# Twelve gate blocks of a hybrid decoder layer moved from the scan to the conv stage: Strassen pairs there, a denser scan here

## The chip, the cores and the metric

The kernel runs on one core of one Trainium2 chip. The metric is the device time of one execution in microseconds; before the change the median of three runs is 2601.65 us (2600.45 to 2602.65). Less is better.

## The reference, cut to what matters

One layer of a decoder works on 1024 prompt tokens and 8 sample tokens, 1032 columns in all, at model width 1024. A combined projection of the normed input gives the inputs of three mixers and their gates:

```
sc_b, sc_c, sc_x, z, xbc, dt_raw, q, gates = split(rmsnorm(x) @ w_in)
y_a = (sc_b * conv3(sc_c * sc_x)) @ w_sc_out
xs, B, C = split(silu(conv4(xbc) + bias))
y_ssd, state = chunked_scan(xs, softplus(dt_raw), a, B, C)      # 8 chunks of 128 tokens, 4 groups of 8 heads
y_b = group_rmsnorm((y_ssd + d * xs) * silu(z)) @ w_ssm_out
y_c = attention(q, mem_k, mem_v) @ w_attn_o
x += (sigmoid(gates) split in three, times y_a, y_b, y_c, summed) @ w_merge_o
x += (silu(n @ w_gate) * (n @ w_up)) @ w_down,  n = rmsnorm(x);   then a final rmsnorm
```

What the change touches is `gates`: 3072 columns of `w_in`, which are 24 blocks of 128, each followed by a sigmoid.

## The kernel before, in words

**Layout.** Activations lie transposed, 128 features by 1032 tokens, as eight pairs of tiles: a rounded fp32r part and the fp32r rest. Each weight block is split the same way, and each product is three matmuls (high by high, high by low, low by high).

**Plain block.** `gemm` (L180) makes 128 output columns: 8 k-steps of 3 matmuls of 3 column stretches of 344, so 72 matmuls at L192. At some k-steps (`marks`, L185) it calls `tick` (L168), which pops one piece of work from the queue `pend` and issues it; `pace[0]` (L178) sets how many pieces a block takes: 3, at k-steps 0, 2 and 5. `run_next` (L138) runs the next block from its queues, and loads the raw weights of the one after it first.

**Strassen pair.** `strassen` (L271) makes two blocks at once from seven products over half the k-range and half the tokens: 7 x 4 k-steps x 3 x 2 stretches of 258, so 168 matmuls at L236. VectorE makes sums of the weights, ScalarE and VectorE split them (L223, L224), and copies and additions join the products (L288 to L318). The sums of the activations (`xforms`) are made once.

**Order of the stages around the change.** First come the norm and six pairs of z blocks beside the memory keys (`z_pair`, L691). Then, at L1138 to L1158, come the *conv inputs*: eleven pairs of xbc blocks and one z pair, L1144. `xbc_pair` (L670) evicts the pair, runs the width-4 conv on VectorE (L595 to L601) and SiLU on ScalarE. Then the Strassen tiles close and the *scan* opens (L1164). Plain blocks are the main work there: a queue `fillers` of eight short-conv channels with three blocks each (`sc_step`, L603) and eight q blocks, and a queue `gates` of the 24 gate blocks (`gate_step`, L646). The 160 pieces of the scan stand in `pend`: per group 3 to load, 27 for the head and the chunks, 1 that loads z, 4 that multiply by z, 2 empty ones and 3 of the group norm, 40 in all.

**One chunk of the scan** is three pieces. p1 (`first`, L755) transposes B and x (L761, L765), multiplies C and B (L762), masks (L767, L770) and scales (L772, L776). p2 (`third`, L811) adds to the state (L815, L821), decays it on GpSimd (L828), works on a sample token (`s_step`, L873) and has ScalarE prepare the next decay matrix `r` (`prep`, L739: eight activations L742, then exp L743). p3 (`second`, L781) makes the output (L789 to L806). The matrix `r` is loaded by a broadcasting DMA of 512 KB, issued by SyncE (L736) two chunks ahead, into one of three tiles; loads, stores and weights share SyncE's queue, in order. Between two groups, `z_pieces` (L944) and `group_norm` (L973; psny L965, x L980, store yb_d L983) free the tiles into which the next group's x is loaded (L1183).

A Tile scheduler fixes each engine's order of instructions when the kernel is built, by its own estimate; it can move a piece's instruction a little later among the plain matmuls.

After the scan, the queue `gates` goes on into the *attention stage* (L1396 to L1443): what is left of the gate blocks, then three rounds of eight output blocks (`out_part`, L1420), beside the 69 pieces of the attention. These load 16 cache tiles `kc` (L1252) and their `qb` (L1249) through two buffers.

Of the kernel before, what the change touches and what calls it, by code (L numbers as in the profile page):

```python
# [11 lines left out]
AF = mybir.ActivationFunctionType  # L12
# [5 lines left out]
P = 128  # L18
# [3 lines left out]
TT = T + NS  # L22
# [15 lines left out]
C_SCB, C_SCC, C_SCX, C_Z, C_XBC, C_DT, C_Q, C_G = 0, 1024, 2048, 3072, 5120, 8192, 8224, 9248  # L38
# [3 lines left out]
def tile_kernel(ctx: ExitStack, tc, a, o):  # L42
    nc = tc.nc
    V, S, G, PE, SY = nc.vector, nc.scalar, nc.gpsimd, nc.tensor, nc.sync
# [22 lines left out]
    def dram(name, shape):  # L67
        return dp.tile(shape, F32, tag=name, name=name)

    def act_tile(part, name, dt=F32R, shape=(P, TT)):  # L70
        return ap_.tile(list(shape), dt, tag=part, name=name)
# [49 lines left out]
    def load_raw(src, name):  # L121
        raw = wp.tile([P, 1024], F32, tag="raw", name=name + "r")
        if len(src.shape) == 3:
            in_turn("raw", SY.dma_start(raw.rearrange("p (k c) -> p k c", k=src.shape[1]), src))
        else:
            in_turn("raw", SY.dma_start(raw, src))
        return raw
# [10 lines left out]
    def run_next(*queues):  # L138

        q = [f for d in queues for f in d]  # L140
        (queues[0] or queues[-1]).popleft()
        if len(q) > 1 and isinstance(q[1], Step):
            loaded[q[1].name] = load_raw(q[1].src, q[1].name)
        q[0]()
# [11 lines left out]
    def ev_tile(name, shape=(P, TT + 4), dt=F32):  # L156
        return ev.tile(list(shape), dt, tag="ev", name=name)
# [20 lines left out]
    pace = [3]  # L178
# [19 lines left out]
    def wblock(w, col):  # L198
        return w[:, col : col + P].rearrange("(k p) c -> p k c", p=P)
# [5 lines left out]
    HS = [slice(0, HT), slice(HT, TT)]  # L205
# [3 lines left out]
    def h3(t):  # L209
        return t.rearrange("p (n c) -> p n c", n=2)  # L210
# [125 lines left out]
    gt_d = dram("gt_d", [24, P, TT])  # L336
    mg_d = dram("mg_d", [KD, P, TT])
    xs_d = dram("xs_d", [24, P, TT])
    zs_d = dram("zs_d", [16, P, TT])
# [16 lines left out]
    w_in = a["w_in"][0]  # L356
# [12 lines left out]
    with tc.tile_pool(name="p0", bufs=1) as p0:  # L369
# [39 lines left out]
        def par(key, i):  # L409
            return prm[:, PC[key] + i : PC[key] + i + 1]  # L410
# [90 lines left out]
    def small(name):  # L501
        return pd_.tile([P, W], F32, tag=name, name=name)

    x0, mx, u, z, z2, q = (small(n) for n in ("x0", "mx", "u", "z", "z2", "q"))
# [141 lines left out]
    def gate_step(i):  # L646
        def s():
            ps = proj(C_G + i * P, f"g{i}")
            t = ev_tile(f"g{i}")
            S.activation(t3(t), flat(ps), AF.Sigmoid)  # L650
            S.dma_start(gt_d[i], t[:, :TT])

        return [Step(wblock(w_in, C_G + i * P), f"wg{i}", s)]

    def xbc_conv(ct, u, name):
        G.memset(u[:, 0:3], 0.0)
        G.tensor_copy(tail_xc[:, ct // 8, :, ct % 8], u[:, T : T + 11])
        acc = ev_tile("a" + name)
        conv(acc, u, h_xc, "xcw", ct, 24, 4, par("scb", ct))
        S.activation(acc[:, :TT], acc[:, :TT], AF.Silu)  # L660
        S.dma_start(xs_d[ct], acc[:, :TT])
# [8 lines left out]
    def xbc_pair(c1, c2, after_t3=None):  # L670
        us = []

        def outs():
            us.extend([pa_["u"](f"u{c1}"), pa_["u"](f"u{c2}")])
            return us[0][:, 3 : 3 + HT], us[0][:, 3 + HT : 3 + TT], None, us[1][:, 3 + HT : 3 + TT]

        pa = strassen(
            wblock(w_in, C_XBC + c1 * P), wblock(w_in, C_XBC + c2 * P), xforms, f"X{c1}", pa_["s"], outs,
            after_t3=after_t3,
        )  # L680
        xbc_conv(c1, us[0], f"x{c1}")
        S.activation(h3(us[1][:, 3 : 3 + HT]), pa, AF.Copy, scale=-1.0)
        xbc_conv(c2, us[1], f"x{c2}")
# [4 lines left out]
        S.activation(t3(t), flat(ps), AF.Silu)  # L688
        S.dma_start(zs_d[i], t[:, :TT])

    def z_pair(i):  # L691
        os = []

        def outs():
            os.extend([pa_["u"](f"z{i}"), pa_["u"](f"z{i + 1}")])
            return os[0][:, HS[0]], os[0][:, HS[1]], None, os[1][:, HS[1]]

        pa = strassen(
            wblock(w_in, C_Z + i * P), wblock(w_in, C_Z + (i + 1) * P), xforms, f"Z{i}", pa_["s"], outs
        )  # L700
        S.activation(os[0][:, :TT], os[0][:, :TT], AF.Silu)
        S.dma_start(zs_d[i], os[0][:, :TT])
        S.activation(os[1][:, HS[1]], os[1][:, HS[1]], AF.Silu)
        S.activation(h3(os[1][:, HS[0]]), pa, AF.Silu, scale=-1.0)
        S.dma_start(zs_d[i + 1], os[1][:, :TT])


    ssd = ExitStack()
# [230 lines left out]
    def z_load(g, t, hold):  # L939
        zs = act_tile(("ah", "al")[t % 2], f"zs{g}{t}", F32)  # L940
        SY.dma_start(zs, zs_d[g * 4 + t])
        hold[t] = zs

    def z_pieces(g, xg, hold):  # L944
        def piece(t):
            zs = hold.pop(t)
            V.tensor_mul(xg[t], xg[t], zs)
            if t == 0:
                hold["q"] = ev_tile(f"sqa{g}")
            sqa = hold["q"]  # L950
            if t == 0:
                S.activation(sqa[:, :TT], xg[t], AF.Square)
            else:
                S.activation(zs, xg[t], AF.Square)
                V.tensor_add(sqa[:, :TT], sqa[:, :TT], zs)
            if t + 2 < 4:
                z_load(g, t + 2, hold)

        return [lambda t=t: piece(t) for t in range(4)]

    def norm_chunk(sqa, i, n, r, v, name):

        c = slice(i * CW, (i + 1) * CW)
        ps = sm_ps(f"psn{name}{i}")
        PE.matmul(ps[:, :CW], ones, sqa[:, c], start=True, stop=True)  # L965
        V.tensor_scalar(v[:, c], ps[:, :CW], 1.0 / n, EPS, op0=ALU.mult, op1=ALU.add)
        S.activation(sqa[:, c], v[:, c], AF.Sqrt)
        V.reciprocal(r[:, c], sqa[:, c])
        V.tensor_mul(sqa[:, c], r[:, c], r[:, c])
        V.scalar_tensor_tensor(sqa[:, c], v[:, c], -0.5, sqa[:, c], op0=ALU.mult, op1=ALU.mult)  # L970
        V.scalar_tensor_tensor(r[:, c], sqa[:, c], 1.5, r[:, c], op0=ALU.add, op1=ALU.mult)

    def group_norm(g, xg, hold):  # L973
        def piece(i):
            if i == 0:
                hold["r"], hold["v"] = ev_tile(f"nr{g}"), ev_tile(f"nv{g}")
            norm_chunk(hold["q"], i, 512, hold["r"], hold["v"], f"y{g}")
            if i == NCH - 1:
                for t in range(4):
                    V.scalar_tensor_tensor(  # L980
                        xg[t], xg[t], par("ssn", g * 4 + t), hold["r"][:, :TT], op0=ALU.mult, op1=ALU.mult
                    )
                    SY.dma_start(yb_d[g * 4 + t], xg[t])  # L983

        return [lambda i=i: piece(i) for i in range(NCH)]

    def q_rows():
# [9 lines left out]
    pa_ = {"u": ev_tile, "s": lambda nm: ev_tile(nm, (P, 1024))}  # L997
# [4 lines left out]
    xforms = {  # L1002
        "B11": [tuple(t[:, HS[0]] for t in xn[k]) for k in range(4)],
        "B21": [tuple(t[:, HS[0]] for t in xn[k + 4]) for k in range(4)],
        "B22": [tuple(t[:, HS[1]] for t in xn[k + 4]) for k in range(4)],
        "T3": [tuple(t[:, HS[1]] for t in xn[k]) for k in range(4)],
        "T1": [], "nT2": [], "T4": [],
    }
# [128 lines left out]
    pa_["s"] = lambda nm: pxa.tile([P, 1024], F32, tag="s", name=nm) if nm[-1] == "a" else ev_tile(nm, (P, 1024))  # L1137
    xbc_pair(17, 21)  # L1138
    xbc_pair(0, 1)
    xbc_pair(2, 3)  # L1140
    xbc_pair(4, 5)
    xbc_pair(6, 7)
    xbc_pair(8, 9)
    z_pair(14)  # L1144
    xbc_pair(10, 11)
    xbc_pair(12, 13)
    xbc_pair(14, 15)
    rb = ev_tile("rb")
    SY.dma_start(rb[:, :TT], r_d.to_broadcast([P, TT]))
# [13 lines left out]

    pool["ssd"] = ssd.enter_context(tc.tile_pool(name="ssd", bufs=2))  # L1164
    gates = deque()
    for i in range(24):
        gates.extend(gate_step(i))
    fillers = deque()
    for ct in range(8):
# [3 lines left out]
    for g in range(GROUPS):  # L1173
        xg, bcg, hold = [], [], {}

        def load_group(g=g, xg=xg, bcg=bcg):
            for i, part in ((16, "ah"), (20, "al")):
                t = act_tile(part, f"bc{i}{g}", F32)
                SY.dma_start(t, xs_d[i + g])
                bcg.append(t)  # L1180
            for i in range(4):
                t = act_tile(("ah", "al")[i % 2], f"x{g}{i}", F32)
                SY.dma_start(t, xs_d[g * 4 + i])  # L1183
                xg.append(t)

        pieces = ssd_pieces(g, xg, bcg)
        pend.extend([load_group, None, lambda g=g, bcg=bcg: bc_rows(g, bcg)])
        pend.extend(pieces[:-3])
        pend.append(lambda g=g, hold=hold: [z_load(g, t, hold) for t in range(2)])
        pend.extend(pieces[-3:])  # L1190
        pend.extend(z_pieces(g, xg, hold) + [None] * 2 + group_norm(g, xg, hold))
    while pend:
        run_next(fillers, gates)


    assert not fillers
# [412 lines left out]
    for j in range(0, NF, 2):  # L1609
        s1, s2, pa = hidden_pair("g", j)  # L1610
# [3 lines left out]
        u1, u2, pa = hidden_pair("u", j)  # L1614
# [143 lines left out]
```

## Time and profile before

| what | us |
|---|---|
| median of 3 runs | 2601.65 |
| the profiled execution: its time / its span | 2603.75 / 2601.7 |
| TensorE busy / VectorE / ScalarE / GpSimd | 2521.7 / 1466.5 / 936.6 / 197.9 |
| mean granted TensorE clock | 0.988 |
| conv inputs, nine pairs, 314.7 to 496.8 | 182.1 |
| scan with its plain blocks, 540.5 to 1296.2 | 755.7 |
| DMA share in the scan | 0.60 |

The time of the profiled execution stands 2.1 above the median and its span 2.05 below that time. Times in the views are from the start of the span. A row of a view reads: start, duration, engine, line, operation, output <- inputs, partitions x elements; in brackets the idle time just before it and what ended it. "PE" is TensorE, "DVE" VectorE, "ACT" ScalarE, "POOL" GpSimd, "SPq" the DMA issues of SyncE. Durations of neighbouring matmuls overlap, so the distance of starts is their price. In a view of stages, each engine has its busy time and its count in brackets, and the row ends with the granted clock, the DMA share and GB/s.

### The profile page before, as it was taken

How to read it: one execution, taken by the hardware profiler on the slowest of the kernel's cores; microseconds unless marked ns; L12 is line 12 of the kernel's file. 1: busy time of each engine (PE TensorE's matmuls, PEld its weight loads, DVE VectorE, ACT ScalarE, POOL GpSimd, SP SyncE). 2: the span in 40 equal slices, each digit the busy share in tenths (PEclk: the TensorE clock that was granted, in tenths of full speed). 3: DMA queues.
4: the chain of work that ended last, by engine and by line, in shares of the span. 5: the costliest groups of instructions: out<-in, count | busy, mean ns of one | idle time of the engine just before them, and what ended most of it. 6: DMA issues, size and time to landing. Idle time of an engine off the chain costs nothing.

```text
span 2601.7 us, 42760 instructions
## 1 busy us (share of the span) xinstructions
PE 2521.7 (97%) x18037; PEld 2453.8 (94%) x18037; DVE 1466.5 (56%) x2037; ACT 936.6 (36%) x1434; POOL 197.9 (8%) x211
## 2 busy tenths in 40 slices
PE   7999999999998999999999999999989999999998
PEld 5899999999998999999999898999979999999998
DVE  5844586866667655555566633444784445454316
ACT  6643444553232235354342322213343333341202
POOL 0000000013213123023000000000010000000000
PEclk9999999999999999999999999999989999999999
DMA  6244333376556755665487757854322222265211
GB/s 190 94 138 156 124 104 106 123 206 148 154 157 138 161 185 160 176 196 150 133 292 243 273 175 252 299 173 144 122 73 82 74 90 66 82 212 163 66 41 66
DMA packets 391422, 389.31 MB, mean 150 GB/s; under 512 B 15622, under 2 KB 337782, under 8 KB 391223
## 3 DMA queue, kind: packets, MB, share of 16 engines
q1 hardware_dynamic: 372654, 335.74, 43.4%
q10 hardware_dynamic: 18577, 50.84, 5.1%
q8 instruction: 142, 2.33, 0.4%
q14 instruction: 49, 0.40, 0.0%
HBM read 280.41 MB, written 106.34 MB: 149 GB/s over the span
## 4 chain that ended last, share of the span: by engine, by line
PE 68%; DMA 5%; DVE 4%; issue 1%; ACT 1%; SPq 0%; POOL 0%; ACTq 0%; DVEq 0%; POOLq 0%
PE ps_g L192 10%; PE po L192 10%; PE pd L192 8%; PE ps_scc L192 4%; PE pm L1535 4%; PE ps_q L192 4%; PE ps_scx L192 3%; PE ps_scb L192 3%; DMA kc<-in_cache_mem_k_dram 1%; PE py L797 1%; PE pss L815 1%; PE po L789 1%; DMA r<-ac_d 1%; PE u20m L236 1%; PE g20m L236 1%
## 5 line engine op out<-in xcount | busy, mean ns | idle before, releaser
L1658 DVE TENSOR_TENSOR x<-pd,x 128x1032 f32<-128x1032 f32 x24 | 29.5, 1231 | 131.4 <-PE pd L192 131.4
L742 ACT ACTIVATE r<-r,acum 128x128 f32<-128x128 f32 x256 | 78.9, 391 | 36.2 <-DMA r<-ac_d 34.8
L1424 DVE TENSOR_TENSOR gt<-po,gt 128x1032 f32<-128x1032 f32 x24 | 29.5, 1230 | 70.4 <-PE po L192 69.1
L776 POOL TENSOR_TENSOR xdd<-xdt,decst 128x512 f32<-128x512 f32 x32 | 46.6, 1456 | 268.1 <-DVE xdt L772 268.1
L1583 POOL TENSOR_TENSOR x<-x,x 128x516 f32<-128x516 f32 x4 | 8.9, 2235 | 635.8 <-DVE x L1502 635.8
L598 DVE SCALAR_TENSOR_TENSOR ax<-u,prm,ax 128x1024 f32<-128x1024 f32 x44 | 56.4, 1281 | 0.3 <-ACT ax L595 0.3
L882 POOL TENSOR_TENSOR st<-st,xb 128x512 f32<-128x512 f32 x32 | 43.8, 1368 | 36.2 <-DVE xb L876 34.0
L769 ACT COPY bT<-bp 128x128 f32<-128x128 f32 x32 | 8.5, 264 | 105.4 <-DVE cbm L767 105.4
L770 DVE TENSOR_TENSOR r<-r,cbm 128x1024 f32<-128x1024 f32 x32 | 39.1, 1222 | 8.6 <-ACT r L743 8.0
L806 DVE SCALAR_TENSOR_TENSOR x<-x,dpar,yt 128x128 f32<-128x128 f32 x128 | 37.5, 354 | 10.1 <-ACT yt L804 9.2
L828 POOL TENSOR_TENSOR s<-s,cdec 128x512 f32<-128x512 f32 x28 | 39.1, 1398 | 46.1 <-DVE s L821 29.6
L821 DVE TENSOR_TENSOR s<-pss,s 128x512 f32<-128x512 f32 x28 | 19.3, 688 | 38.8 <-PE pss L815 38.8
L815 PE MATMUL pss<-xdd,bT 128*128 128x512 f32 x64 | 33.8, 610 | 6.6 <-ACT bT L769 6.5
L879 POOL TENSOR_TENSOR st<-st,es 128x512 f32<-128x512 f32 x32 | 36.6, 1143 | 20.3 <-DMA st<-in_state_ssm_dram 16.7
L797 PE MATMUL py<-r,xdt 128*64 128x128 f32 x512 | 35.0, 279 | 1.5 <-issue 1.5
L767 DVE TENSOR_TENSOR cbm<-bp,tri 128x128 f32<-128x128 f32 x32 | 9.3, 290 | 45.3 <-PE bp L762 45.2
L743 ACT ACTIVATE r<-r 128x1024 f32<-128x1024 f32 x32 | 33.9, 1059 | 0.7
L793 DVE TENSOR_TENSOR yt<-po,ea 128x512 f32<-128x512 f32 x28 | 19.2, 686 | 25.7 <-PE po L789 25.7
L797 PEld LDWEIGHTS py<-r,xdt 128*64 128x64 f32 x512 | 27.3, 136 | 5.8 <-issue 2.4
L1263 ACT ACTIVATE pr<-psa,mx 128x256 f32<-128x256 f32 x32 | 14.9, 472 | 48.8 <-DVE mx L1261 48.8
L1253 DVE TENSOR_TENSOR kc<-kc,qb 128x1024 f32<-128x1024 f32 x16 | 19.6, 1224 | 22.0 <-DMA kc<-in_cache_mem_k_dram 21.9
L1542 DVE TENSOR_TENSOR x<-pm,xT 128x516 f32<-128x516 f32 x16 | 11.1, 695 | 36.2 <-PE pm L1535 36.2
(7961 smaller groups left out, 8684.3 us busy)
## 6 DMA issues: line engine op xcount, KB each, us to landing
gt<-gt_d SPq DMA_DIRECT2D x32, 516.0 KB
r<-ac_d SPq DMA_DIRECT2D x32, 512.0 KB
gt_d<-g ACTq DMA_DIRECT2D x24, 516.0 KB
mg_d<-gt SPq DMA_DIRECT2D x24, 516.0 KB
mg<-mg_d SPq DMA_DIRECT2D x24, 516.0 KB
xs_d<-ax ACTq DMA_DIRECT2D x22, 516.0 KB
hr<-h_d SPq DMA_DIRECT2D x22, 516.0 KB
zs_d<-z ACTq DMA_DIRECT2D x16, 516.0 KB
```

Of the source, the lines that this page charges most:

```text
L192: PE.matmul(ps[:, n, :CW], wt[:, ks], x[:, n * CW : (n + 1) * CW], start=(k == 0 and i == 0), stop=(k == nk - 1 and i == 2),)
L236: PE.matmul(ps[:, n, :HC], wt[:, ks], x[:, n * HC : (n + 1) * HC], start=(start and kt == 0 and i == 0), stop=(kt == 3 and i == 2), skip_g ...
L598: V.scalar_tensor_tensor(acc[:, :T], u[:, j : j + T], w[j], acc[:, :T], op0=ALU.mult, op1=ALU.add)
L742: S.activation(r[:, h, :], r[:, h, :], AF.Relu, scale=-1.0, bias=acum[:, c, h0 + h : h0 + h + 1])
L770: V.tensor_tensor(r, r, bc(cbm.unsqueeze(1), [P, HPG, P]), op=ALU.mult)
L776: G.tensor_tensor(b3(xdd, HPG), b3(xdt, HPG), bc(decst[:, c, hs].unsqueeze(2), [P, HPG, 64]), op=ALU.mult)
L797: PE.matmul(py[hp : hp + 64, (h // 2) * P : (h // 2 + 1) * P], xdt[:, h * 64 : (h + 1) * 64], r[:, h, :], start=True, stop=True,)
L806: V.scalar_tensor_tensor(xg[t][:, cs], xg[t][:, cs], dpar[:, g * 4 + t : g * 4 + t + 1], yt[:, t, :], op0=ALU.mult, op1=ALU.add,)
L815: PE.matmul(pss, bT, xdd, start=True, stop=True)
L828: ins = G.tensor_tensor(b3(s_new, HPG), b3(state["s"], HPG), bc(cdec[:, c, hs].unsqueeze(2), [P, HPG, 64]), op=ALU.mult,)
L882: G.tensor_tensor(st, st, xb, op=ALU.add)
L1535: PE.matmul(ps[:, n, :HC], wt[:, ks], x[:, half * HT + n * HC : half * HT + (n + 1) * HC], start=(k == 0 and i == 0), stop=(k == KD - 1 an ...
```

## The change

`z_pair` becomes a general `plain_pair`, and `gate_pair` uses it. Gate blocks 0 to 11 are made by six Strassen pairs, put between the pairs of conv inputs; the z pair moves ahead of xbc pair 8, 9. The queue of the scan starts at gate 12, and while the scan's pieces last, a plain block takes four of them (k-steps 0, 2, 4, 6).

```diff
+    def plain_pair(col, dst, i, nm, func):
...
+        pa = strassen(
+            wblock(w_in, col + i * P), wblock(w_in, col + (i + 1) * P), xforms, f"{nm}{i}", pa_["s"], outs
+        )
+        S.activation(os[0][:, :TT], os[0][:, :TT], func)
+        S.dma_start(dst[i], os[0][:, :TT])
+        S.activation(os[1][:, HS[1]], os[1][:, HS[1]], func)
+        S.activation(h3(os[1][:, HS[0]]), pa, func, scale=-1.0)
+        S.dma_start(dst[i + 1], os[1][:, :TT])
+
     def z_pair(i):
...
+        plain_pair(C_Z, zs_d, i, "Z", AF.Silu)
+
+    def gate_pair(i):
+        plain_pair(C_G, gt_d, i, "G", AF.Sigmoid)
...
     xbc_pair(0, 1)
+    gate_pair(0)
     xbc_pair(2, 3)
+    gate_pair(2)
     xbc_pair(4, 5)
+    gate_pair(4)
     xbc_pair(6, 7)
+    z_pair(14)
     xbc_pair(8, 9)
-    z_pair(14)
+    gate_pair(6)
     xbc_pair(10, 11)
+    gate_pair(8)
     xbc_pair(12, 13)
+    gate_pair(10)
     xbc_pair(14, 15)
...
-    for i in range(24):
+    for i in range(12, 24):
         gates.extend(gate_step(i))
...
+    pace[0] = 4
     while pend:
         run_next(fillers, gates)
+    pace[0] = 3
```

With three pieces to a block, the 160 pieces last 53 1/3 of the 56 blocks of `fillers` and `gates`; with four they last 40 of the 44 that are left. One block more runs beside the rows of q, and then one gate block (before) or three (after) run beside the first attention pieces.

## The prediction on record

> **What bounds the kernel now.** I read the page first: the busy shares, the slices, and the chain of waits by engine.
>
> ```profile
> span 2601.7 us, 42760 instructions
> ...
> PE 2521.7 (97%) x18037; PEld 2453.8 (94%) x18037; DVE 1466.5 (56%) x2037; ACT 936.6 (36%) x1434; POOL 197.9 (8%) x211
> ...
> PE   7999999999998999999999999999989999999998
> ...
> DVE  5844586866667655555566633444784445454316
> ...
> PE 68%; DMA 5%; DVE 4%; issue 1%; ACT 1%; SPq 0%; POOL 0%; ACTq 0%; DVEq 0%; POOLq 0%
> ```
>
> TensorE is busy 97% and carries the chain. Only fewer matmul columns, or less of its idle time, can shorten the kernel. Next I asked for the busy time of the two stages that the change touches, of three chunks of the scan, and of a stretch around a long wait.
>
> ```profile
> 314.70:496.80 182.10, 182.10 (x1515) 182.10 (x1514) 144.32 (x196) 90.95 (x106) 4.91 (x32) 1.00 0.34 111
> ...
> 540.50:1296.20 755.70, 744.19 (x4964) 713.72 (x4965) 451.99 (x650) 286.21 (x492) 173.98 (x147) 0.99 0.60 160
> ...
> 581.88:627.20 45.32, 45.32 (x316) 42.95 (x316) 30.31 (x49) 16.25 (x35) 16.82 (x14) 1.00 0.67 156
> ...
> 842.00:852.00 10.00, 7.83 (x44) 6.58 (x44) 3.94 (x4) 7.89 (x20) 5.62 (x4) 0.67 0.37 102
> ```
>
> In the conv inputs TensorE has no idle time (182.10 of 182.10), while VectorE is at 79% and ScalarE at 50%. In the scan it idles 11.5 us out of 755.7, VectorE is at 60%, ScalarE at 38%, GpSimd at 23%, the DMA engines at 0.60. So both stages are bound by TensorE, and the scan has covers for its latencies that the change will make thinner.
>
> **Price of a plain block and of a pair.** From the chain of waits, in order of time:
>
> ```profile
> 581.88 3.06 PE ps_scc L192 x18
> ...
> 589.98 0.86 PE pss L815 x2
> ...
> 596.98 3.06 PE ps_scx L192 x18
> ...
> 1248.22 25.50 PE ps_g L192 x162
> ```
>
> 162 plain matmuls without a break take 25.50 us, 157.4 ns each, so a block of 72 is 11.33 us. From 581.88 to 596.98 is one chunk of the scan with one block: 15.10 us, of which 11.33 are the block and 3.77 the chunk's own matmuls. The pairs I take from the rows of their tiles; "first and last start" stands after the comma.
>
> ```profile
> L236 PE MATMUL X0m<-xnh,X0Ah x16: 277/282/288, 314.7 to 325.6; 128*128 128x258 f32 x16
> ...
> L236 PE MATMUL Z14m<-xnh,Z14Ah x16: 277/282/287, 415.8 to 426.8; 128*128 128x258 f32 x16
> ...
> L236 PE MATMUL X10m<-xnh,X10Ah x16: 277/282/288, 436.1 to 447.0; 128*128 128x258 f32 x16
> ...
> L236 PE MATMUL X18m<-xnh,X18Ah x16: 277/282/288, 496.8 to 507.7; 128*128 128x258 f32 x16
> ```
>
> Nine pairs from 314.7 to 496.8 are 20.23 us each. The z pair, which is built just as a gate pair, takes 436.1 - 415.8 = 20.3 between two conv pairs: nothing of its neighbours is lost.
>
> **The change part by part, and the sum.**
>
> *Six gate pairs added to the conv inputs:* 6 x 20.23 = **+121.4**. What else they bring lies beside TensorE: VectorE has 144.32 / 9 = 16 us of work per conv pair and less in a gate pair, which has no conv, so its share falls. The sigmoid is not in the same table as SiLU: in the built order the conv inputs go from 0 to 12 table loads.
>
> ```profile
> L650 ACT ACT_TABLE_LOAD  x13: 1283/1283/1283, 1010.3 to 1296.0; - x13
> ```
>
> 12 x 1.28 = 15.4 us more on a ScalarE that idles half of this stage: cost 0, and at most 15.4 if each load stood in front of a copy that TensorE waits for.
>
> *Twelve plain blocks removed from the scan:* 12 x 11.33 = **-136.0**. The 160 pieces keep their own matmuls. The two terms together give -14.6, which is the gain if no wait changes.
>
> *The start of the scan.* These rows are of four engines' orders in time:
>
> ```profile
> 540.50 0.73 PE L192 MATMUL ps_scc<-xnh,wscc0h 128*128 128x344 f32 x3 [1.67 <-ACT u L682]
> ...
> 546.83 1.00 SPq L736 DMA_DIRECT2D r<-ac_d  x2
> ...
> 556.53 1.57 ACT L742 ACTIVATE r<-r,acum 128x128 f32<-128x128 f32 x5 [8.52 <-DMA r<-ac_d]
> ...
> 561.25 0.40 ACT L742 ACTIVATE r<-r,acum 128x128 f32<-128x128 f32 x1 [1.35 <-DMA r<-ac_d]
> ...
> 562.97 1.06 ACT L743 ACTIVATE r<-r 128x1024 f32<-128x1024 f32 x1
> ...
> 564.06 1.23 DVE L770 TENSOR_TENSOR r<-r,cbm 128x1024 f32<-128x1024 f32 x1 [7.97 <-ACT r L743]
> ...
> 565.39 1.09 PE L797 MATMUL py<-r,xdt 128*64 128x128 f32 x16 [1.53 <-issue]
> ```
>
> The first `r` can be loaded only when the conv stage's tiles are released, lands 9.7 us later, and goes through ScalarE and VectorE; the first py can start 24.9 us after the scan's first matmul. Before it stand 144 plain matmuls, 22.66 us; with 0.7 for the chunk's transposes and the breaks (24.89 - 22.66 - 1.53) that leaves the 1.53 us of waiting. In the built order of the changed kernel 108 stand there, 17.0 us, with the breaks 17.7. ScalarE's order gets better there by 1.75 us (the activation at 561.25 on the second `r`, with its wait of 1.35, no longer stands ahead of the first exp), so py is ready at 23.1: a wait of 5.4, **+3.9**. A wait of that size also costs clock, as two waits show, one of 2.3 us before 663 and one of 6.5 us before 844:
>
> ```profile
> 663.87 5.65 PE ps_scb L192 x26
> ...
> 831.22 11.59 DMA r<-ac_d
> ...
> 844.17 2.04 PE pss L815 x2
> 846.21 3.98 PE ps_scc L192 x18
> ```
>
> After 844 the granted clock over ten microseconds is 0.67; the pss takes 2.04 us (0.86 at 589.98) and 18 plain matmuls 3.98 (2.83 by 157.4 ns): 2.3 us lost. After 663, 26 matmuls take 5.65 (4.09): 1.6 lost. I take **+1.7**, nearer to the smaller; ends 0 and 3.4. [...]
>
> *The three passages between groups.* The rows: first norm product and last x' of the second passage, then of the third.
>
> ```profile
> 906.85 0.74 PE L965 MATMUL psny<-sqa,ones 128*128 128x344 f32 x2
> ...
> 936.01 0.17 DVE L857 TENSOR_TENSOR xds<-x,dts 128x8 f32<-128x8 f32 x1 [1.18 <-DMA x<-xs_d]
> ...
> 1090.19 0.74 PE L965 MATMUL psny<-sqa,ones 128*128 128x344 f32 x2
> ...
> 1123.31 0.33 PE L765 MATMUL xp<-ident,x 128*128 128x128 f32 x1 [0.61 <-DMA x<-xs_d]
> ```
>
> From the first norm product to the landing of the next group's last x, a chain of VectorE, a store and a load takes 29.2 and 33.1 us. By pace alone the cover would shrink. But the scheduler has moved the last two transposes: in the built order 169, 184 and 169 plain matmuls stand between, against 171, 171 and 184 before, that is 26.6 to 29.0 us plus 2.7 of the pieces' own matmuls. So the cover stays nearly the same; I take +0.5 each, **+1.5**, since py now comes right behind, with 5 or 6 matmuls (0.9 us) for the VectorE operation between them. Ends 0 and 3 x 5.
>
> *Waits within the groups.* From the waits of the scan, in total, times, longest:
>
> ```profile
> PE pss L815 <- ACT bT L769: 6.5, 1, 6.5
> ...
> PE xp L765 <- DVE yt L802: 2.3, 1, 2.3
> ...
> ACT r L742 <- DMA r<-ac_d: 34.8, 6, 17.8
> ```
>
> Both waits of TensorE hang on a late `r`: ScalarE stands before its activations, and what is queued behind it (weight casts, bT) comes late. With the clock they cost 12.7 now (6.5 + 2.3, and 2.3 + 1.6 in slow matmuls behind them). A chunk goes from 15.10 to 0.75 x 11.33 + 3.77 = 12.3 us, so all covers shrink by a fifth. The load of `r` is issued about four pieces ahead, 20 us before and 16 after, and 11.59 is the longest landing on the chain. In SyncE's built order the group's last `r` now stands ahead of the loads that wait for VectorE. I take **-3**, with ends -12.7 (both gone) and +12.7 (twice as many). VectorE is no bound: 30.31 us for three chunks and three blocks is 10.1 a piece, and with a quarter less of a block (3.2 us of weight and short-conv work) 9.3 in 12.3.
>
> *The hand-over and the attention.* Here two gate blocks take the place of two output blocks beside the first `kc` loads.
>
> ```profile
> 1329.26 0.74 PE L192 MATMUL po<-b00h,wo00h 128*128 128x344 f32 x3 [2.92 <-ACT b00h L162]
> ...
> 1320.00:1460.00 140.00, 129.25 (x824) 125.08 (x822) 99.75 (x137) 53.08 (x100) 0.00 (x0) 0.99 0.81 275
> ```
>
> TensorE idles 10.75 us there at a DMA share of 0.81. A gate block loads no gate and no partial sum, as an output block does, which relieves it; but in the built order the loads of the first output block now stand behind five `kc` loads in SyncE's queue. I take 0; ends -6 and +8.
>
> **Sum:** 121.4 - 136.0 + 3.9 + 1.7 + 1.5 - 3 = -10.5, of the profiled execution's 2603.75: 2593.2. The median of the runs stands 2.1 lower: 2601.65 - 10.5 = **2591**.
>
> **Rivals.**
>
> *All covered.* The start's wait is half of what I take, and the two waits on `r` go altogether: -14.6 + 2.8 + 1.5 - 10 = -20.3, **2581**. For it: the new order of `r` on SyncE. Against: the start hangs on a release that does not move.
>
> *The gain is eaten.* Each of the 32 chunks loses 0.3 us, since between two pieces there are 18 matmuls (2.83 us) instead of mostly 27 (4.25), and VectorE must finish yt in this gap before the next xp. What can stop it there is GpSimd:
>
> ```profile
> L598 DVE SCALAR_TENSOR_TENSOR sacc<-u,prm,sacc x8: 1274/1282/2367, 571.0 to 878.5; 128x1024 f32<-128x1024 f32 x8
> ...
> L879 POOL TENSOR_TENSOR st<-st,es 128x512 f32<-128x512 f32 x32 | 36.6, 1143 | 20.3 <-DMA st<-in_state_ssm_dram 16.7 <-DVE xb L876 3.5
> ```
>
> The same instruction takes 1282 ns mostly and 2367 once: 1.09 us more, about one GpSimd operation (1143). Where such a block falls into the gap, TensorE waits about a quarter of it: 32 x 0.3 = 9.6, so -0.9, **2601**. [...]
>
> *Slower: `r` comes late in each group.* The wait of 6.5 us at 844, with its 2.3 of clock and lengthened by the 4 us by which the cover shrinks, comes once in each of the four groups: 4 x 12.8 - 12.7 = +38.5, so 2601.65 - 14.6 + 5.6 + 1.5 + 38.5 = **2633**. It decides from the point where a load of `r` lands later than 16 us after its tile is free; half of it, two such groups, gives 2607. For it: the DMA share in the chunk rises from 0.67 by up to a fifth. Against: one landing of 11.6 is the longest seen.
>
> *The change does not do what it says:* no; in the built order 18 plain matmuls stand between the pieces, and the six pairs between the conv pairs.
>
> **How the numbers follow.** Forecast (2585 to 2599) 0.45; all covered 0.2; gain eaten 0.15; slower 0.2. A measurement of this kernel can tell about 0.2% from no change, 5.2 us: faster is under 2596.4, slower over 2606.9. The forecast puts 0.37 of its 0.45 below 2596.4. With "all covered" faster has 0.57; the rest of the forecast, "eaten" and a little of the half-sized slower case give 0.23; slower 0.2. The range goes from 2579 (all covered, and the attention's relief) to 2611 (a little over two late groups), which leaves out about 0.17.
>
> **What would show it.** Gate pairs at 20.2 to 20.3 us and no idle time in the conv inputs; a scan stage of about 755.7 - 136.0 + 4.1; the first py with a wait near 5.4 and the clock down behind it; waits before the x' transposes under 2 us. Wrong would be: conv pairs longer than 20.3 (the table loads), waits for `r` in every group, or many short waits at xp spread over the chunks.

## The result, and the profile after

The changed kernel takes 2613.81 us (median of four runs, 2610.54 to 2617.63) against 2601.05 of the kernel before on the same chip: ratio 1.0047, 95% interval 1.0035 to 1.006. It is slower by 12.8 us, half a per cent; 2591 was forecast. Its profiled execution took 2617.63 us with a span of 2615.9, so 13.9 and 14.2 above the profiled execution of before.

The page of the changed kernel, the lines that answer to those of before:

```profile
span 2615.9 us, 43180 instructions
...
PE 2514.7 (96%) x18181; PEld 2445.7 (93%) x18181; DVE 1507.0 (58%) x2091; ACT 958.6 (37%) x1472; POOL 200.7 (8%) x211
...
PE   7999999999899989899989999999989999999998
...
PE 82%; DVE 8%; DMA 6%; ACT 2%; issue 2%; ACTq 0%; SPq 0%; POOL 0%; DVEq 0%
```

TensorE is busy 7.0 us less than before (2514.7 against 2521.7) and the span is 14.2 longer: the work has shrunk, the idle time has grown. In the slices, four of the eleven in the middle (the 11th to the 21st) are an 8, where before it was one.

The two stages after the conv inputs, first the scan up to the transposes of q's rows (psqr), then from there to the first product of the merge (pm), before:

```profile
540.50:1295.20 754.70, 743.19 (x4956) 712.88 (x4957) 450.99 (x649) 285.23 (x491) 173.98 (x147) 0.99 0.60 160
1295.20:1769.00 473.80, 460.56 (x2970) 442.60 (x2969) 240.68 (x293) 134.35 (x221) 0.00 (x0) 0.99 0.71 239
```

and after:

```profile
664.20:1280.70 616.50, 590.09 (x3947) 558.44 (x3948) 428.15 (x627) 236.98 (x448) 175.82 (x147) 0.98 0.64 171
1280.70:1783.90 503.20, 483.81 (x3114) 466.40 (x3112) 250.98 (x302) 143.88 (x230) 0.00 (x0) 0.98 0.68 230
```

The second number of a row is its length, then comes TensorE's busy time with its matmuls. The counts of matmuls turn these rows into a balance: the scan has lost 14 blocks of 72, the attention has gained 2, at 11.33 us each; the conv stage runs from its first pair to the scan's first matmul (314.7 to 540.5 before, 315.3 to 664.2 after) and has six pairs more at 20.23.

| stage | before | after | change | by the work | lost |
|---|---|---|---|---|---|
| conv inputs | 225.8 | 348.9 | +123.1 | +121.4 | 1.7 |
| scan | 754.7 | 616.5 | -138.2 | -158.7 | 20.5 |
| attention, to pm | 473.8 | 503.2 | +29.4 | +22.7 | 6.7 |
| sum | | | +14.3 | -14.6 | 28.9 |

So the pairs and the blocks are worth 14.6 as counted, but 28.9 us are lost around them, most of it in the scan. The pairs themselves keep their price: the row of the first conv pair, whose first start is 315.3, and that of the sixteenth,

```profile
L236 PE MATMUL X0m<-xnh,X0Ah x16: 277/282/287, 315.3 to 326.2; 128*128 128x258 f32 x16
...
L236 PE MATMUL X18m<-xnh,X18Ah x16: 277/282/288, 619.3 to 630.3; 128*128 128x258 f32 x16
```

lie 304.0 us apart for 15 pairs, 20.27 each. The waits of TensorE in the scan (us in total, times, longest):

```profile
PE pss L822 <- ACT bT L776: 14.5, 2, 7.6
PE xp L772 <- DVE yt L809: 6.0, 3, 5.1
PE py L804 <- issue: 4.4, 1, 4.4
```

One is the start, at 686. The three others, at 773, 932 and 1088, stand at the same place in three groups: in the last chunk, just ahead of the passage to the next group. The chain of waits around the second:

```profile
912.92 10.15 DMA r<-ac_d
...
923.09 0.40 ACT r L749
923.49 0.95 ACT r L750
924.44 2.05 ACT r L749 x7
...
928.48 0.95 ACT wscc6h L152
...
929.46 1.23 DVE wscc6l L153
...
931.73 0.21 DVE cbm L774
...
931.97 0.28 ACT bT L776
...
932.38 2.05 PE pss L822 x2
934.42 7.33 PE ps_scx L192 x36
```

And ScalarE's own order there:

```profile
909.72 2.45 ACT L749 ACTIVATE r<-r,acum 128x128 f32<-128x128 f32 x8
923.09 0.40 ACT L749 ACTIVATE r<-r,acum 128x128 f32<-128x128 f32 x1 [10.92 <-DMA r<-ac_d]
923.40 1.04 ACT L750 ACTIVATE r<-r 128x1024 f32<-128x1024 f32 x1
```

A chunk's `r` takes eight relus (L749) and one exp (L750). The eight relus at 909.72 are those of the group's last `r`, r_7. The exp of r_7 follows only at 923.40, because the built order has put one relu of the *next* group's r_0 in between, and its load has only been issued at 912.92. Behind this relu stand the exp, a weight cast, VectorE's part of that weight, the product cbm and the copy bT, on which pss waits. The wait has its price in clock too: 36 matmuls take 7.33 us where 5.67 is usual, and the granted clock from 932.3 to 942.0 is 0.71.

### The profile page after: what moved, and what is told of

Read it like the earlier page. It is cut to its first block, busy times and chain, and to the rows that moved or that the text cites. A ratio compares the mean times of both kernels' runs of the same rounds, so it can differ in the third digit from the quotient of the medians.

```text
span 2615.9 us, 43180 instructions
## 1 busy us (share of the span) xinstructions
PE 2514.7 (96%) x18181; PEld 2445.7 (93%) x18181; DVE 1507.0 (58%) x2091; ACT 958.6 (37%) x1472; POOL 200.7 (8%) x211
## 4 chain that ended last, share of the span: by engine, by line
PE 82%; DVE 8%; DMA 6%; ACT 2%; issue 2%; ACTq 0%; SPq 0%; POOL 0%; DVEq 0%
PE po L192 12%; PE pd L192 8%; PE ps_g L192 4%; PE pm L1550 4%; PE ps_q L192 3%; PE ps_scx L192 3%; PE ps_scc L192 3%; DMA kc<-in_cache_mem_k_dram 2%; PE ps_scb L192 2%; DMA r<-ac_d 1%; PE py L804 1%; PE pss L822 1%; PE Z12m L236 1%; PE Z4m L236 1%; PE ps_z L192 1%
## 5 line engine op out<-in xcount | busy, mean ns | idle before, releaser
L749 ACT ACTIVATE r<-r,acum 128x128 f32<-128x128 f32 x256 | 78.9, 392 | 37.0 <-DMA r<-ac_d 36.4
L1439 DVE TENSOR_TENSOR gt<-po,gt 128x1032 f32<-128x1032 f32 x24 | 29.5, 1230 | 80.4 <-PE po L192 80.3
L598 DVE SCALAR_TENSOR_TENSOR ax<-u,prm,ax 128x1024 f32<-128x1024 f32 x44 | 56.3, 1279 | 0.2
L822 PE MATMUL pss<-xdd,bT 128*128 128x512 f32 x64 | 34.7, 625 | 14.5 <-ACT bT L776 14.5
L886 POOL TENSOR_TENSOR st<-st,es 128x512 f32<-128x512 f32 x32 | 39.5, 1234 | 16.5 <-DMA st<-in_state_ssm_dram 16.5
L750 ACT ACTIVATE r<-r 128x1024 f32<-128x1024 f32 x32 | 33.8, 1057 | 0.5
L895 DVE TENSOR_TENSOR xc<-bcb,st 128x512 f32<-128x512 f32 x32 | 22.7, 711 | 18.9 <-POOL st L889 17.5
L1479 DVE TENSOR_TENSOR gt<-po,gt 128x1032 f32<-128x1032 f32 x8 | 9.9, 1232 | 40.4 <-PE po L192 40.4
```

The source lines that it names most:

```text
L598: V.scalar_tensor_tensor(acc[:, :T], u[:, j : j + T], w[j], acc[:, :T], op0=ALU.mult, op1=ALU.add)
L749: S.activation(r[:, h, :], r[:, h, :], AF.Relu, scale=-1.0, bias=acum[:, c, h0 + h : h0 + h + 1])
L822: PE.matmul(pss, bT, xdd, start=True, stop=True)
L886: G.tensor_tensor(st, st, bc(es[:, g * 4 : g * 4 + 4, b : b + 1], [P, 4, P]), op=ALU.mult)
```

## The experiments

The theories at first: A, the three waits come from the place of that relu in ScalarE's order; B, `r` lands late because the denser scan loads the DMA queues, and what needs it next would wait anyway. Each ratio below is against the kernel before on the same chip. A profiled execution can stand some us from the median of its kernel (e4 5.4 below, e6 5.5 above, e9 4.9 below); so stages are compared by rows, kernels by medians.

**e1: only the order on ScalarE.** The relus of the next r_0 must stand behind the last bT of the old group.

```diff
-            state["bT"] = S.copy(bT, bp[:, :P]).ins
+            state["bT"] = passed["bT"] = S.copy(bT, bp[:, :P]).ins
...
-            prep(0)
+            if passed:
+                with tc.issue_after(passed["bT"]):
+                    prep(0)
+            else:
+                prep(0)
```

> The changed kernel with one edge of order added: the relus of the next group's first r stand behind bT of the old group's last chunk on ScalarE, where three of four passages had one of them ahead of the exp of r_7. Theory A (the three long waits of the scan come from that place in ScalarE's order, not from the load itself): the waits of 5.1, 7.6 and 6.9 us before xp 773, pss 932 and pss 1088 go, with 2.1, 2.9 and 2.9 us of slow matmuls behind them, 27.5 us in all: 2613.8 - 27.5 = 2586, clearly under the kernel before. Theory B (the DMA is the limit: r lands 10 us after its issue because the scan is denser, so whatever needs it next waits instead): the waits move to the first chunk of the next group, 2606 to 2614.

Measured: 2611.45 us, ratio 1.0043 (1.0028 to 1.0058). The number falls into B's range, but the trace doesn't show what B says. The waits on bT are gone, as A has it, and no wait on `r` has taken their place; others have, 40 to 70 us later:

```profile
PE xp L774 <- DMA x<-xs_d: 9.3, 3, 4.0
PE py L806 <- issue: 4.9, 1, 4.9
PE psny L978 <- DVE nv L979: 4.3, 2, 3.2
```

They lie in the passage itself, which the prediction had costed at 0.5 each. VectorE's order at the first one:

```profile
809.93 0.17 DVE L866 TENSOR_TENSOR xds<-x,dts 128x8 f32<-128x8 f32 x1 [7.40 <-DMA x<-xs_d]
812.84 0.17 DVE L866 TENSOR_TENSOR xds<-x,dts 128x8 f32<-128x8 f32 x1 [2.74 <-DMA x<-xs_d]
...
815.20 0.51 DVE L979 TENSOR_SCALAR nv<-psny 128x344 f32<-128x344 f32 x1
```

It is the same thing on another engine. Two products of 0.17 us that belong to the next group wait 10.1 us for their x, and the old group's norm (nv) stands behind them; only when the norm is done are the tiles free into which the other two x are loaded. In the changed kernel the wait on bT, which came first, had hidden this: VectorE stands 28.5 us at xds there in all, and 47.4 here. (The expectation took 2.9 us of slow matmuls behind the third wait; the chain at 1088 shows 1.8, so A's sum should read 26.4.)

**e2: the same edge in the kernel before.**

> The kernel before with the same edge of order. Theory A: its two waits of 6.5 and 2.3 us go, with 2.3 and 1.6 us of slow matmuls: 2601.6 - 12.7 = 2589; the change would then be worth what is left between this and the changed kernel with the edge, a few us. Theory B: 2598 to 2602. If only the wait of 6.5 hangs on the order (the row of 2.3 shows exp r_7 ahead of the relus already), 2593.

Measured: 2591.66 us, ratio 0.997 (0.9957 to 0.9983): 8.8 us from one edge of order, between A's two numbers. Its scan takes 743.7 us where the kernel before takes 754.7. The wait of 6.5 has gone, and that of 2.3 is 1.1. At three pieces to a block the passages bear the early xds, at four they don't.

**e3: the denser scan alone.** No gate pairs; 24 plain gates, four pieces to a block.

```diff
-    gate_pair(0)
...
-    for i in range(12, 24):
+    for i in range(24):
         gates.extend(gate_step(i))
```

> The denser scan alone: no gate pairs, all 24 gates as plain blocks, four pieces to a block; 16 gate blocks are then left for the attention. Theory A (the pairs pay as counted, the pieces' covers are what is lost): the time is the changed kernel's plus the 14.6 us that the pairs save: 2613.8 + 14.6 = 2628, less some 2 for the conv stage's losses, 2626; the scan shows waits of 5 to 8 us at the same three passages. Theory C (the pairs lose in the conv stage, by twelve table loads or by taking tiles, and the scan is as good as before): 2602 or below.

Measured: 2620.51 us, ratio 1.0076 (1.0059 to 1.0094). The row of its scan, and its waits there:

```profile
539.50:1153.30 613.80, 588.50 (x3948) 557.09 (x3949) 428.34 (x629) 236.88 (x448) 176.22 (x147) 0.98 0.64 172
```

```profile
PE pss L822 <- ACT bT L776: 12.8, 2, 7.9
PE xp L772 <- DVE yt L809: 7.4, 3, 6.6
```

Without any pair the scan has nearly the length and the waits of the changed kernel (616.5, with 14.5 and 6.0): the pairs don't disturb it, the pace does. It came out 5.5 below the 2626 of theory A. The stages account for it: the scan is 2.7 shorter, and the attention, 634.2 us with 14 blocks more than in the kernel before (473.8), loses 1.7 where the changed kernel loses 6.7; with 16 gate blocks left, its longest wait for pTl is 2.2 instead of 10.5.

**e4: three pieces to a block for the first 24 pieces.** The first group is less dense, and two gate blocks instead of four are left for the attention.

```diff
+    pieces_left = len(pend) - 24
     while pend:
+        pace[0] = 3 if len(pend) > pieces_left else 4
         run_next(fillers, gates)
```

> The changed kernel with the first 24 pieces of the scan at three to a block and the rest at four, so that two blocks fewer are left beside the attention. Theory A: the first wait for py falls from 4.4 to some 1.5 us and its slow matmuls from 3.0 to at most 1.3 (-4.6); in the built order the first passage has exp r_7 ahead of the relus of r_0, so its wait of 5.1 with 2.1 of slow matmuls goes too (-7.2): 2602. The two other passages keep their waits of 7 us. Theory B: 2609 (only the start gains).

Measured: 2604.06 us, ratio 1.0013 (1.0003 to 1.0022). A's 2602 is near, but it is made up in another way. The start's wait falls to 0.6 and the first of the three waits goes. And the row of the attention

```profile
1290.80:1764.60 473.80, 462.85 (x2970) 445.55 (x2969) 247.45 (x300) 134.30 (x222) 0.00 (x0) 0.99 0.71 240
```

is that of the kernel before (473.80): with two gate blocks left instead of four, the 6.7 us lost there don't arise. Against this, the first passage has a wait of 3.5 for x, and two waits of 4.9 and 5.4 stay.

**e5: the kc products begin with the second head.** The loss in the attention is mostly one wait, at 1350. Its chain in the changed kernel:

```profile
1326.07 8.29 DMA kc<-in_cache_mem_k_dram
...
1343.07 5.47 DMA kc<-in_cache_mem_k_dram
...
1348.66 1.22 DVE kc L1268
1349.89 0.34 DVE pTl L1376
...
1350.37 0.76 PE psv L1386
```

The loads of kc go one after the other, each into the tile that the product before has freed, and VectorE stands at each product until its load has landed (4.37, 1.59 and 4.15 us before the products at 1334.45, 1340.56 and 1348.66). pTl, for which psv waits 10.5 us, stands behind them.

```diff
-                pieces.append(both(*fs, *aside(), *late) if fs else both(*late, *aside()))
+                kc = aside() if h else ()
+                pieces.append(both(*fs, *kc, *late) if fs else both(*late, *kc))
```

> The changed kernel with the sample scores (the loads of kc and their products on VectorE) left out of the first head's pieces and begun with the second head's. Theory A (VectorE stands in line behind a product whose kc lands late, and pTl behind it: the 10.5 us before psv at 1350): the wait goes, and the attention loses what it loses in the kernel before, 26.8 us by matmul counts and not 33.9: 2613.8 - 7 = 2607. Theory B (it is the blocks: too many gate blocks stand before the first output block, so the loads of its inputs come late whatever kc does): the wait moves to po, 2611 to 2614.

Measured: 2607.34 us, ratio 1.0026 (1.0017 to 1.0035), as theory A has it. The attention's row, with the same matmuls as in the changed kernel:

```profile
1276.90:1772.30 495.40, 484.04 (x3114) 465.89 (x3112) 250.38 (x302) 144.36 (x230) 0.00 (x0) 0.99 0.68 234
```

495.4 for 503.2. This loss too is an instruction that waits for a load and stands in an engine's order ahead of one that TensorE needs. Theory B is not all wrong: the first output block now waits 3.6 for its input (2.9 in the kernel before), and a wait of 3.7 for sc_s, a product of the late kc, is new.

**e6: five pairs, three pieces to a block at the start and around the passages, edge on ScalarE.** At this point theory C was that the chain norm, store, load of x is simply longer than four pieces to a block can cover; D, that the steady chunks lose as well.

```diff
+        at_ = 160 - len(pend)
+        pace[0] = 3 if at_ < 8 or at_ % 40 < 6 or (at_ % 40 >= 34 and at_ < 150) else 4
```

> Five gate pairs, the edge of order, and three pieces to a block where a chain of latency must be covered (the first 8 pieces of the scan and 12 around each passage between groups), four elsewhere; two gate blocks are left beside the attention, as in the kernel before. Theory C (the pairs pay 2.43 us each, steady chunks bear four pieces, and only the start, the passages and the hand-over do not): 2591.7 - 5 x 2.43 = 2579.5, with 1 us lost in the conv stage 2580.5. Theory D (steady chunks lose too, some 0.3 us each of the two dozen dense ones): 2587.

Measured: 2590.71 us, ratio 0.9963 (0.9951 to 0.9976). C's number is missed by 10, and what D says is not in the trace either: its steady chunks show no wait over 0.7 us. Even with three pieces to a block the first passage waits 3.6 for x, and in the second an operand of the scan's own, u, comes 3.4 late behind an xds whose x VectorE awaits for 14.2. A longer cover doesn't cure an instruction in the wrong place.

**e7: a shorter way from the norm to the load.** This kernel leaves out the mean square of the group's norm, so it does not compute the layer; it is only there to time the passage.

```diff
-            norm_chunk(hold["q"], i, 512, hold["r"], hold["v"], f"y{g}")
-            if i == NCH - 1:
+            if i == 0:
                 for t in range(4):
...
-                        xg[t], xg[t], par("ssn", g * 4 + t), hold["r"][:, :TT], op0=ALU.mult, op1=ALU.mult
+                        xg[t], xg[t], par("ssn", g * 4 + t), hold["q"][:, :TT], op0=ALU.mult, op1=ALU.mult
```

> The changed kernel with the edge of order, and with the mean square of the group's norm left out (the outputs are scaled by the parameter and the squares' tile instead, and stored when the first norm piece comes). It takes out 24 products of 0.16 us, 3.8 us of TensorE. Theory C (at a passage the chain norm, store of y, release of the tile, load of the next x is longer than what four pieces to a block leave as cover): the waits for x (9.3) and in the norm (4.3) go with some 4 us of slow matmuls: 2611.4 - 21.7 = 2590. Theory B (the loads of x are late in the queue whatever releases their tile): the waits for x stay: 2603.

Measured: 2576.87 us, ratio 0.9907 (0.9894 to 0.9921), 13 below C's number. The scan takes 581.2 us where e1's takes 611.1, and TensorE idles 14.5 less in it, about as C has it. But TensorE is also busy 15.4 us less there, where C had counted 3.8 for the products and 4 for slow matmuls, and the attention is 3.4 shorter. No wait for x of 0.3 us or more is left, and those in the norm are gone, so the passage does hang on the way from norm to load and not on the queue of x. This doesn't yet tell C from an early xds: both make that way long, and VectorE still stands 43.6 us at xds, with no norm behind it.

**e8: two pairs, edge on ScalarE, four pieces to a block in the last group alone.**

```diff
-    pace[0] = 4
     while pend:
+        at_ = 160 - len(pend)
+        pace[0] = 3 if at_ < 120 else 4
```

> Two gate pairs, the edge of order, three pieces to a block in three groups and four in the last one, which no passage follows; two gate blocks are left beside the attention. Theory C: no new wait, so 2591.7 - 2 x 2.43 = 2587. If a pair is not worth what the rows say (conv stage, table loads), 2591 or more.

Measured: 2591.66 us, ratio 0.9962 (0.9949 to 0.9974), no better than e2. That is the number of the alternative, but not its reason, for the pairs cost what was counted: from the first pair to the scan it takes 265.8 us where e2 takes 225.5, 40.3 for two pairs. The scan gives back 43.9 of 45.3, and the attention takes 475.3 where e2's takes 470.8, with the same matmuls.

**e9: both edges.** The products xds of the next group must stand behind the old group's last norm product (theory E: again the order, not the length of the chain).

```diff
-                    V.scalar_tensor_tensor(
+                    passed["y"] = V.scalar_tensor_tensor(
...
+                with tc.issue_after(passed["y"]):
+                    s_prep()
```

> The changed kernel with the edge on ScalarE and a second one on VectorE: the products xds of the next group's x stand behind the old group's last norm product, where two of them stood ahead of the norm and waited 7.4, 13.5 and 11.3 us for x in the run with the first edge alone. Theory E (at a passage it is again an instruction of the next group that stands too early in an engine's order): the norm starts some 10 us earlier, the waits for x (9.3) and in the norm (4.3) go with some 5 us of slow matmuls: 2611.4 - 18.6 = 2593. Theory C (the chain of norm, store and load is itself too long for four pieces to a block): about half of it stays, 2602.

Measured: 2591.76 us, ratio 0.9964 (0.9954 to 0.9974): E's 2593, not C's 2602. Its rows, with the same matmuls as the changed kernel, and its waits in the scan:

```profile
662.90:1250.90 588.00, 582.24 (x3947) 552.39 (x3948) 431.50 (x627) 237.31 (x448) 176.13 (x147) 1.00 0.68 179
1250.90:1753.30 502.40, 484.23 (x3115) 467.02 (x3113) 251.05 (x302) 143.80 (x230) 0.00 (x0) 0.98 0.68 231
```

```profile
PE py L806 <- issue: 3.7, 1, 3.7
...
PE xp L774 <- DMA x<-xs_d: 0.6, 1, 0.6
```

The same work takes 588.0 us instead of 616.5, at a clock of 1.00 instead of 0.98 and at a DMA share of 0.68 instead of 0.64. More traffic in less time, and no wait over 0.6 at any passage: that rules out B. The attention's loss (502.4 against 503.2) is untouched, as it should be. The edge on VectorE was not run without the one on ScalarE.

**e10: both edges in the kernel before.**

> The kernel before with both edges. With the first alone its passages show no wait of TensorE over 1.1 us, so theory E and theory C both say 2591; over 2595 would mean that the second edge does harm of its own. It is the base against which the gate pairs are to be judged.

Measured: 2589.85 us, ratio 0.9966 (0.9954 to 0.9979), as expected. Its rows:

```profile
540.30:1282.50 742.20, 739.36 (x4955) 709.94 (x4956) 450.23 (x651) 288.13 (x493) 175.97 (x147) 1.00 0.60 163
1282.50:1756.10 473.60, 461.54 (x2971) 444.06 (x2969) 241.03 (x293) 134.02 (x221) 0.00 (x0) 0.99 0.70 240
```

**e11: six pairs, both edges, late kc, and the first eight pieces at three to a block.**

> The changed kernel (six pairs) with both edges, the kc products begun with the second head, and three pieces to a block for the first eight pieces. If the three causes add up (passages, hand-over, start): 2593 - 7 - 5 = 2581, the kernel before with both edges less four of the six pairs' gain. If the hand-over's cost belongs to the number of gate blocks left, 2588.

Measured: 2587.36 us (2586.61 to 2589.45), ratio 0.9952 (0.9939 to 0.9964). It is the fastest kernel with the whole computation, 13 us under the kernel before, but the causes don't add up to 2581; 2588, the number of the alternative, is nearer. Its rows, and its longest waits from the scan to the third head:

```profile
663.00:1265.10 602.10, 594.69 (x4020) 563.85 (x4021) 430.36 (x629) 242.64 (x452) 177.05 (x147) 1.00 0.66 177
1265.10:1753.50 488.40, 472.84 (x3043) 455.18 (x3041) 248.15 (x300) 139.62 (x226) 0.00 (x0) 0.99 0.69 235
```

```profile
PE xp L774 <- DMA x<-xs_d: 4.6, 3, 3.6
PE psp L1377 <- DVE sc_s L1278: 4.5, 1, 4.5
```

The start no longer waits; but the third passage waits 3.6 for x again, and in the attention a wait of 4.5 for sc_s, which belongs to the late kc, and one of 3.0 for the output block's input stand for the 10.7 that is gone. The rows of the third passage show order once more, now on SyncE: the stores of y (first at 1123.62) stand behind bcb's load, which waits until 1122.63 for bc_d to land. Here the first store is issued 2.95 us after VectorE has begun on y (1120.67), in e9, where the stores stand ahead of bcb, 1.3; so this may be some 1.6 of the 3.6. No run tried it.

**e12: a seventh pair on top.**

> The same with a seventh gate pair, so that little more than one gate block is left beside the attention: 2.4 us less than with six if the pairs go on paying, 2578.6; 2583 to 2585 if the hand-over loses some 4 us with so few blocks, as it did with two pairs and a dense last group.

Measured: 2591.82 us, ratio 0.9968 (0.9956 to 0.9979): 4.5 slower than with six by the medians; the two intervals overlap, so this only says that a seventh pair gains nothing. Little more than one gate block is left, the first output block waits 6.1 for its inputs, and the attention takes 477.6 with 145 matmuls less than in e11, two blocks, by which it should take 465.7. The hand-over does lose with so few blocks, but 12 us and not the 4 that were expected.

## Why the prediction was wrong, point by point

- **Six gate pairs, +121.4**: right. The conv stage grew by 123.1; of the 1.7 above, 0.6 is 15 pairs at 20.27 for 20.23, and a wait of 1.3 of the last conv pair for u makes up most of the rest. There VectorE stood 1.4 us at wscc0l, the low part of the scan's first weight, before it came to that u. The 12 table loads of the conv inputs, 15.4 us of ScalarE, cost nothing that the trace shows: from 315.30 to 639.50 TensorE is busy 323.65 us of 324.20.
- **Twelve plain blocks, -136.0**: right, as the balance of the stages shows (14 fewer in the scan, 2 more in the attention).
- **The start, +3.9 and +1.7**: right in its mechanism. The wait is 4.4 instead of the 5.4 taken, and its slow matmuls cost 3.0 instead of 1.7, as the chain shows against 1.02 (py at 1097.46) and 2.83 (18 at 157.4 ns), both at a granted clock of 1.00, where from 686.2 to 693.2 it is 0.57:

```profile
686.28 1.98 PE py L804 x16
688.26 4.86 PE ps_scx L192 x18
```

  Together +5.9 to the wait of before, where 5.6 was taken; that the two errors cancel is luck. The end of 3.4 for the slow matmuls was the author's estimate, and no run shows it: the most behind one wait of this scan is the 3.0 here.
- **Waits within the groups, -3 with ends of 12.7**: this is the step that failed. The prediction looked at the lead of the loads of `r` and at their order on SyncE, took 11.59 as the longest landing, and concluded that `r` comes in time. The landings stay below that: 9.6, 10.2 and 10.1 us at the three places. What it left out is ScalarE's order: one relu of the next group's r_0 ahead of the exp of r_7, in three passages, where the kernel before had such an order in two and waited long in one. The three waits (5.1, 7.6, 6.9) with their slow matmuls (2.1, 2.9, 1.8) cost 26.4 instead of 12.7: +13.7 where -3 was taken. That is also more than the end of +12.7. With it the sum comes out: -14.6 + 1.7 in the conv stage, 5.9 at the start, 13.7 here and 6.7 in the attention make +13.4 of the +14.3 in the table.
- **The three passages, +1.5**: right in the changed kernel by an accident, wrong as a step. The built order has the cover that was counted, but e1 shows 9.3 and 4.3 us of waits there as soon as the waits ahead of them are gone, and e9 that their cause is xds ahead of the norm on VectorE. The row of xds stood in the prediction with its wait of 1.18; what stood behind it on its engine was not asked.
- **Hand-over and attention, 0 with ends of -6 and +8**: the size was off, within its ends: +6.7. The prediction had seen the kc loads, and looked for their harm on the output block's inputs; e5 shows that it comes through VectorE's queue.
- **The rivals.** "All covered" (2581) was reached by no run with the whole computation: 2591.8 in e9, with the start and the attention still lost, and 2587.4 in e11. Its sum takes 10 for two waits that cost 12.7 in the step before it. "The gain is eaten" by VectorE and GpSimd did not happen: xp's waits on yt in all steady chunks come to 0.9 us in e9. "Slower: r late in each group" had the right place, though it counted four and there are three passages, with 8.8 each, and the wrong condition: the load doesn't land later than 16 us, it is waited for too early. Its half, 2607, was the nearest of the rivals' numbers.

**Where the expected gain went.** Against the kernel before with the same two edges (e10), six pairs and four pieces to a block change the time by +1.9 us (e9, medians), and by -2.5 with the start and kc mended as well (e11), which is about what can't be told from nothing. By the rows of e9 and e10: conv 123.0 for 121.4, the scan -154.2 for 14 blocks of 158.7, the attention +28.8 for 22.7; 12.2 of the 14.6 are lost: 1.6 in the conv stage, 4.5 in the scan (the start's wait, 3.7 where e10's is 1.1, and its clock), 6.1 in the attention. e9's profiled execution stands 4.9 below its median; by the medians 16.5 are lost. So the two edges, which gain 22 us in the changed kernel and 10.6 in the one before, explain 16.7 of the 28.9 by the rows and some 11 of 27.4 by the medians: about half is the order on ScalarE and VectorE at the passages, and most of the rest goes at the two ends of the scan. What stays open: why late kc and a slower start together gain 4.4 us (e9 to e11) where 12 were expected. The waits that took their place are named above; their causes were not tried.

## What to carry to other kernels

When a stage is made denser, read each engine's order at the joints of the stage, not only the lead of the loads: ask of every instruction that waits for a load what stands behind it. Here a short instruction of the next stage, put early because it was free to go, held up the last of the old stage for as long as its load took, 4 to 14 us for 0.2 to 1.2 us of work. Such waits can hide each other, so one edge alone may show little (2.4 us in e1) and two together much (22 us in e9); judge by the waits that are left in the trace.

## What the runs showed of the hardware

Waits of 4.4, 5.1, 7.6 and 6.9 us were each followed by slow matmuls that cost 3.0, 2.1, 2.9 and 1.8 us: in these four the price in clock does not grow with the length of the wait. The ten microseconds around each, with the granted clock in the fourth place (length, TensorE busy, matmuls, clock, DMA share, GB/s):

```profile
680.00:690.00 10.00, 5.62 (x35) 0.77 0.76 180
770.00:780.00 10.00, 6.51 (x27) 0.66 0.70 168
930.00:940.00 10.00, 7.62 (x28) 0.60 0.64 173
1080.00:1090.00 10.00, 3.14 (x12) 0.74 0.61 164
```

A shorter wait of the kernel before has its price as well: 2.25 us, ended at 663.21, were followed by 1.6 us of slow matmuls (26 in 5.65 us, 4.09 by 157.4 ns), at a granted clock of 0.83 from 663 to 673.

In the rows at 923.09 and 809.93 an instruction that had its operand stood behind one that waited for a load. On ScalarE an exp whose operand had been ready since 912 stood until 923.40 behind a relu that waited 10.92 us. On VectorE in e1 nv, whose sums in psny were done at 808.43, began at 815.20, behind two xds that had waited 7.40 and 2.74 us.

In the kernel before, five of the eight products sacc (L598) took 1.27 to 1.28 us. The three others ran beside products of GpSimd and were longer: 1.91 us at 779.84, 1.90 at 825.17, and 2.37 at 878.54, where a GpSimd product of 1.29 us began at the same time.
